# A two-layer decoder trunk on one core: scores of alternating row halves, values as the stationary operand, and gates and branches issued in another order

## The chip, the core and the metric

The kernel runs on one core of a Trainium2 chip. TensorE (PE; PEld is its loading of weights) multiplies, VectorE (DVE) and ScalarE (ACT) do the element-wise work, GpSimd (POOL) a few powers, and SyncE (SP) issues the DMAs. The metric is the device time of one execution in microseconds; lower is better.

## What is computed

Two equal layers over 256 tokens of width 1024, in float32. Cut to what matters here:

```
h    = rms_norm(x);  proj = h @ w_in[l]              # columns of four mixers A, B, C, D, then 4 x 1024 gate columns
yA   = attention over the top 64 keys that an indexer of 8 heads x 32 picks (1 k/v head)
yB   = block attention (one block of 256 keys: plain causal), 4 heads x 64
yC   = g0*compressed + g1*selected blocks + g2*window attention      # 1 k/v head each
yD   = sliding window 128 with a learned sink per head, 2 k/v heads
br_n = y_n @ w_branch[l, n]
x    = x + (sum_n sigmoid(gate_n) * br_n) @ w_out[l]
x    = x + conv_ffn(rms_norm(x))                     # up, causal width-3 convolution, silu * value, down
```

## The kernel before, in words

Every weight matrix comes in chunks of up to 1 MB through three buffers (`raw`); ACT rounds each piece of up to 128x1024 to a short float (`hi`), DVE subtracts it from the original (`lo`), four tiles of each. TensorE then does three fast products per weight tile (`hi` by the high and the low part of the activations, `lo` by the high part), with 128 tokens as the stationary operand and 512 weight columns moving, into PSUM banks `mm0` to `mm3`. The attention itself is in plain float32, which TensorE runs as two records per product.

One layer goes: projections of A, B, D, C; then for each branch n its gate (two halves of 512 columns, 48 fast products each) and its branch product (two halves, 12 each); the output product; up and down of the FFN. While TensorE works on that main stream, the four mixers run beside it: norms, rotations, transposes, and ten calls of `attend` in a layer (A, B and D two each, C four), one for the first 128 queries (t=0, 128 keys) and one for the second (t=1, 256 keys).

`attend` does, for four heads: scores (q as stationary operand, 64 rows of the array per product; heads of even and odd number lie in rows 0 to 63 and 64 to 127) into a bank `sc` for each parity, a maximum on DVE (`attend_max`), exponentials on ACT, transposes of the probabilities through a bank `tr` and copies back (`evac_tr`), and the product with the values. Before, the transposed probabilities are the stationary operand (128x128) and the values (64 columns) move; the result, queries in partitions, is multiplied by 1/denominator on DVE. `y_T` then transposes a mixer's result (four transposes) for the branch product. `indexer` multiplies heads of 32 rows in four row groups, one group after another.

No engine's order is written by hand. Each piece of work is a generator that yields the engine it wants and the values it waits for; `Flow.run` keeps a clock for each engine, prices each instruction with `Eng.cost`, and issues next whatever can start first by these clocks, then by priority. "AV" takes ACT or DVE, whichever is free first. The order is fixed at build time; on the chip each engine works through its own in order. Buffers and banks go round in rings (`mm_r`: 4 banks, `sc_r`: 2, `tr_r`: 2), so an owner must give one back before the next can take it.

Of the kernel before, what the change touches and what calls it, by code (L numbers as in the profile page):

```python
# [9 lines left out]
F32 = mybir.dt.float32  # L10
F32R = mybir.dt.float32r
# [161 lines left out]
class Eng:  # L173
# [6 lines left out]
    def cost(self, m, a, k):  # L180
# [49 lines left out]
def trunk(ctx: ExitStack, tc: tile.TileContext, a, out):  # L230
# [163 lines left out]
    GATES = (0, 1, 2, 3)  # L394
    HID_AT = (0, 1)
    PRIO = (4, 19, 7, 21)
# [6 lines left out]
    for l in range(DEPTH):  # L403
# [7 lines left out]
        for n in GATES:  # L411
            for half in range(2):
# [3 lines left out]
                if (n, half) == HID_AT:  # L416
                    for i in range(2):
                        ap = a["c_cmp_w1"][l, i].rearrange("(c p) h -> p c h", p=128)
                        plan.append(Chunk(ap, (16, 128), []))
                if n == GATES[-1]:  # L420
                    rows_chunk(a["w_branch"][l, n], 0, 2, half * 512, half * 512 + 512)
            if n != GATES[-1]:
# [211 lines left out]
    def attend(t, qT, kblk, kT, vfn, scl, mask, y, needs, sink=None, fin=None, gate=None):  # L634
        nk = 128 * (t + 1)
        Sx = sm = None
        rdf = Fut()
        tx = []
        for par in range(2):
            if par == 0:  # L640
                sxt, sm, sc = yield "PE", needs, [sx_r, sm_r, sc_r]
                Sx = sxt.rearrange("p (h n) -> p h n", h=H)
                mx, nmx, den, es, rd = (sm[k] for k in ("mx", "nmx", "den", "es", "rd"))
            else:
                sc, = yield "PE", [], [sc_r]
            b = 64 * par
            for hh in range(2):
                te = P.matmul(sc[:, hh * nk:hh * nk + nk], qT[b:b + 64, hh, t * 128:t * 128 + 128],
                              kT[b:b + 64, kblk(2 * hh + par), :nk], start=True, stop=True)
            fl.spawn(attend_max(t, sc, te, par, Sx, nk, mask, scl, sink, mx, tx), 8)  # L650
# [14 lines left out]
        fl.spawn(recip(t2, den, rd, gate, rdf), 8)  # L665
        tes = []
        pTt = None
        for g in range(t + 1):
            if g == 0:
                pTt, tb = yield "PE", [te], [pt_r, tr_r]  # L670
                pT = pTt.rearrange("p (h b q) -> p h b q", h=H, b=2)
            else:
                tb, = yield "PE", [], [tr_r]
# [14 lines left out]
        sx_r.give(sxt, tq)  # L688
        ob, = yield "PE", tes, [tr_r]
        op = ob[:, :256].rearrange("p (h d) -> p h d", h=H)  # L690
# [4 lines left out]
        rdb = rd[:, :, None].to_broadcast([128, H, DH])  # L695
        if gate is None:
            yield "DVE", [te, rdf], []
            te = V.tensor_tensor(heads(y)[:, t], op, rdb, op=ALU.mult)
            tr_r.give(ob, te)
        else:  # L700
            otmp, = yield "DVE", [te, rdf], [ot_r]
            te = V.tensor_tensor(otmp, op, rdb, op=ALU.mult)
            tr_r.give(ob, te)
            yield "DVE", [te], []
            te = V.tensor_tensor(heads(y)[:, t], heads(y)[:, t], otmp, op=ALU.add)
            ot_r.give(otmp, te)
        sm_r.give(sm, te)
# [128 lines left out]
    def indexer(t, iqT, ikT, iw, needs, fin, f):  # L836
        nk = 128 * (t + 1)
        mask = tri[:, 256 - nk:]
        ac = acc[t]
        for r4 in range(4):  # L840
            sc, rl = yield "PE", needs, [sc_r, rl_r]
            for g in range(2):
                te = P.matmul(sc[:, g * nk:g * nk + nk], iqT[32 * r4:32 * r4 + 32, g, t * 128:t * 128 + 128],
                              ikT[32 * r4:32 * r4 + 32, 0, :nk], start=True, stop=True)
            yield "ACT", [te], []
            te = A.activation(rl[:, :2 * nk], sc[:, :2 * nk], AF.Relu)
            sc_r.give(sc, te)
            td = te
# [162 lines left out]
    ot_r = Ring([junk[:, :256].rearrange("p (h d) -> p h d", h=H)])  # L1011

# [30 lines left out]
    def nsa_cmp(qT, needs, tvb, cgv, y, y0):  # L1043
# [26 lines left out]
        fl.spawn(cmp_den(tp_, Pv, crd, cgv, crd_f := Fut()), 12)  # L1070
        pTt, tb = yield "PE", [tp_], [pt_r, tr_r]
# [6 lines left out]
        for t in range(NT):  # L1078
            te = P.matmul(tb[:, t * 256:t * 256 + 256], pTt[:, t * 128:t * 128 + 128], vbd.rearrange("p h d -> p (h d)"),
                          start=True, stop=True)  # L1080
        pt_r.give(pTt, te)
        yield "DVE", [te, crd_f], []
        te = V.tensor_tensor(heads(y), tb.rearrange("p (t h d) -> p t h d", t=NT, h=H),
                             crd[:, :, :, None].to_broadcast([128, NT, H, DH]), op=ALU.mult)
# [30 lines left out]
    def merge(mg, ps, rg, te, gate, gf, half, i, old, f):  # L1115
        hs = slice(half * 512, half * 512 + 512)
        for t in range(NT):
            if i == 0:
                yield "DVE", [te, gf], []
# [313 lines left out]
```

## Time and profile before

| | us |
|---|---|
| median of 3 runs | 877.55 (877.33 to 881.88) |
| the profiled execution | 881.64 |
| its span, first to last instruction | 879.8 |
| PE busy | 874.4 (99%) |
| DVE busy | 667.9 (76%) |
| ACT busy | 526.3 (60%) |

The profile is of one execution. "Busy" of PE is modelled from pipelined records: one lasts longer than the time until the next starts, so what a product costs is read from start to start in the timeline.

### The profile page before, as it was taken

How to read it: one execution, taken by the hardware profiler on the slowest of the kernel's cores; microseconds unless marked ns; L12 is line 12 of the kernel's file. 1: busy time of each engine (PE TensorE's matmuls, PEld its weight loads, DVE VectorE, ACT ScalarE, POOL GpSimd, SP SyncE). 2: the span in 40 equal slices, each digit the busy share in tenths (PEclk: the TensorE clock that was granted, in tenths of full speed). 3: DMA queues.
4: the chain of work that ended last, by engine and by line, in shares of the span. 5: the costliest groups of instructions: out<-in, count | busy, mean ns of one | idle time of the engine just before them, and what ended most of it. 6: DMA issues, size and time to landing. Idle time of an engine off the chain costs nothing.

```text
span 879.8 us, 14193 instructions
## 1 busy us (share of the span) xinstructions
PE 874.4 (99%) x5491; PEld 766.2 (87%) x5491; DVE 667.9 (76%) x1301; ACT 526.3 (60%) x895; POOL 34.3 (4%) x31
## 2 busy tenths in 40 slices
PE   9999999999999999999999999999999999999998
PEld 8979887788889999988898888787888999999886
DVE  4779888956768999884457997968476699899642
ACT  5655465555457887764455465646545598888431
POOL 0111002000000000000001111000000000000000
PEclk9999999999999999999999999999999999999999
DMA  7627364235555555555554264542356455565560
GB/s 266 237 87 240 96 239 145 83 127 174 192 176 179 200 191 192 193 168 193 170 172 168 85 205 144 193 144 97 120 184 222 144 192 195 194 201 192 178 215 25
DMA packets 103413, 149.90 MB, mean 170 GB/s; under 512 B 4072, under 2 KB 62258, under 8 KB 103346
## 3 DMA queue, kind: packets, MB, share of 16 engines
q1 hardware_dynamic: 103346, 149.00, 50.6%
q8 instruction: 43, 0.70, 0.3%
q14 instruction: 24, 0.20, 0.1%
HBM read 147.94 MB, written 1.05 MB: 169 GB/s over the span
## 4 chain that ended last, share of the span: by engine, by line
PE 98%; ACT 0%; DMA 0%; SPq 0%; DVE 0%; issue 0%; DVEq 0%
PE mm L212 82%; PE sc L212 8%; PE tr L212 8%; DMA rn<-in_norm_g_dram 0%; ACT f L212 0%; ACT L212 0%; SPq L240 0%; ACT hi L212 0%; DVE x L212 0%; DVEq L1429 0%
## 5 line engine op out<-in xcount | busy, mean ns | idle before, releaser
L212 DVE TENSOR_TENSOR lo<-raw,hi 128x1024 fp32r<-128x1024 f32 (+2 forms) x280 | 328.1, 1177 | 117.2 <-ACT hi L212 113.3
L212 ACT ACTIVATE hi<-raw 128x1024 fp32r<-128x1024 f32 (+2 forms) x280 | 283.3, 1022 | 170.7 <-PE mm L212 143.1
L212 PE MATMUL mm<-hi,ahi 128*128 128x512 f32 (+4 forms) x480 | 178.1, 377 | 0.0
L212 PE MATMUL mm<-hi,alo 128*128 128x512 f32 (+4 forms) x480 | 172.3, 365 | 0.0
L212 PE MATMUL mm<-ahi,hi 128*128 128x256 f32 x640 | 152.3, 279 | 0.0
L212 PE MATMUL mm<-alo,hi 128*128 128x256 f32 x640 | 152.0, 278 | 0.0
L212 PEld LDWEIGHTS mm<-ahi,hi 128*128 128x128 f32 x640 | 120.6, 188 | 0.1
L212 PEld LDWEIGHTS mm<-alo,hi 128*128 128x128 f32 x640 | 120.6, 188 | 0.1
L212 PE MATMUL mm<-lo,ahi 128*128 128x512 f32 (+4 forms) x480 | 118.3, 370 | 0.0
L212 PEld LDWEIGHTS mm<-hi,ahi 128*128 128x128 f32 x480 | 90.7, 189 | 14.9 <-issue 2.7
L212 PEld LDWEIGHTS mm<-hi,alo 128*128 128x128 f32 x480 | 90.8, 189 | 11.2
L212 PEld LDWEIGHTS mm<-lo,ahi 128*128 128x128 f32 x480 | 82.9, 188 | 13.8 <-issue 1.7
L212 PE MATMUL mm<-hi,slotQ 128*128 128x512 f32 x352 | 89.9, 395 | 0.0
L212 PE MATMUL mm<-ahi,lo 128*128 128x256 f32 x640 | 88.1, 278 | 0.0
L212 PEld LDWEIGHTS mm<-ahi,lo 128*128 128x128 f32 x640 | 80.2, 188 | 0.0
L212 PEld LDWEIGHTS mm<-hi,slotQ 128*128 128x128 f32 x352 | 66.1, 188 | 15.3
L212 ACT ACTIVATE f<-f,col 128x256 f32<-128x256 f32 x88 | 48.1, 593 | 14.5 <-DVE f L212 14.0
L212 PE MATMUL mm<-lo,slotQ 128*128 128x512 f32 x176 | 48.7, 395 | 0.0
L212 ACT ACTIVATE f<-f,nmx 128x128 f32<-128x128 f32 (+1 forms) x80 | 35.4, 445 | 9.6 <-DVE nmx L212 9.4
L212 ACT ACTIVATE slotP<-mm,rh 128x512 f32<-128x512 f32 x32 | 20.4, 684 | 33.2 <-PE mm L212 33.0
L212 PE MATMUL sc<-qk 64*128 64x128 f32 (+3 forms) x224 | 39.9, 348 | 0.0
L212 PEld LDWEIGHTS mm<-lo,slotQ 128*128 128x128 f32 x176 | 33.0, 188 | 7.6
(219 smaller groups left out, 1091.7 us busy)
## 6 DMA issues: line engine op xcount, KB each, us to landing
raw<-in_w_up_dram SPq DMA_DIRECT2D x44, 1024.0 KB, 5.0
raw<-in_w_in_dram SPq DMA_DIRECT2D x40, 1024.0 KB, 4.9
raw<-in_w_down_dram SPq DMA_DIRECT2D x20, 1024.0 KB, 4.9
raw<-in_w_out_dram SPq DMA_DIRECT2D x8, 1024.0 KB, 5.2
raw<-in_w_branch_dram SPq DMA_DIRECT2D x6, 1024.0 KB, 5.7
raw<-in_w_in_dram SPq DMA_DIRECT2D x7, 768.0 KB, 6.1
raw<-in_w_in_dram SPq DMA_DIRECT2D x4, 592.0 KB, 4.1
raw<-in_w_in_dram SPq DMA_DIRECT2D x4, 536.0 KB
```

The lines of the kernel that those rows point to most:

```text
L212: fn(*a, **k)
```

## The change

- `attend`: both parities of the scores are issued in one step that takes both `sc` banks, in turn (even, odd, even, odd). The probabilities are divided by the denominator before they are transposed, four instructions on ACT or DVE, which wait for `recip`. The values become the stationary operand (64 columns) and the transposed probabilities move (128 columns); the result has features in partitions, even heads in 0 to 63 and odd heads in 64 to 127, and is copied (or, in C, added) into `y`.
- `y_T` no longer transposes: a copy on ACT and a subtraction on DVE.
- `indexer`: the eight score products in one step, row groups in turn, into four banks (two `sc`, two `tr`).
- `nsa_cmp`: as `attend`, with the same number of products.
- Gates and branches follow a list, `SEQ`: gates 0, 1, 2, then branches 0, 1, 2, then gate and branch 3 by halves. The first gate is written to `mg` itself. Priorities of mixers B, C and D change.
- The planner prices a fast product at 0.446 ns a column, 0.417 before, and divides the price of products in separate strips by their number (`P.side`).

```diff
-                c = 0.417 * n + 2 if a[1].dtype == F32R else 1.67 * max(n, free_size(a[1])) + 2
+                c = 0.446 * n + 2 if a[1].dtype == F32R else 1.67 * max(n, free_size(a[1])) + 2
...
-    GATES = (0, 1, 2, 3)
-    HID_AT = (0, 1)
-    PRIO = (4, 19, 7, 21)
+    SEQ = [("gate", 0, 0), ("gate", 0, 1), ("hidden", 0, 0), ("hidden", 1, 0), ("gate", 1, 0),
+           ("gate", 1, 1), ("gate", 2, 0), ("gate", 2, 1), ("branch", 0, 0), ("branch", 0, 1),
+           ("branch", 1, 0), ("branch", 1, 1), ("branch", 2, 0), ("branch", 2, 1), ("gate", 3, 0),
+           ("branch", 3, 0), ("gate", 3, 1), ("branch", 3, 1)]
+    PRIO = (4, 7, 19, 21)
...
     def y_T(y, yf, yT, f):
-        yT += yield "PE", [yf], [y_r]
-        yield from rows_T(y, [yf], yT[0], 0, f)
+        yT += yield "ACT", [yf], [y_r]
+        te = A.activation(yT[0][0], y, AF.Copy)
+        yield "DVE", [te], []
+        f.t = V.tensor_tensor(yT[0][1], y, yT[0][0].bitcast(F32), op=ALU.subtract)
...
-        for par in range(2):
-            if par == 0:
-                sxt, sm, sc = yield "PE", needs, [sx_r, sm_r, sc_r]
...
-            else:
-                sc, = yield "PE", [], [sc_r]
-            b = 64 * par
-            for hh in range(2):
-                te = P.matmul(sc[:, hh * nk:hh * nk + nk], qT[b:b + 64, hh, t * 128:t * 128 + 128],
+        sxt, sm, *scs = yield "PE", needs, [sx_r, sm_r, sc_r, sc_r]
...
+        for hh in range(2):
+            for par in range(2):
+                b = 64 * par
+                te = P.matmul(scs[par][:, hh * nk:hh * nk + nk], qT[b:b + 64, hh, t * 128:t * 128 + 128],
...
+        for h in range(H):
+            eng, _ = yield "AV", [rdf], []
+            if eng == "ACT":
+                tn.append(A.activation(Sx[:, h, :nk], Sx[:, h, :nk], AF.Copy, scale=rd[:, h:h + 1]))
+            else:
+                tn.append(V.tensor_scalar(Sx[:, h, :nk], Sx[:, h, :nk], rd[:, h:h + 1], None, op0=ALU.mult))
...
-        for h in range(H):
+        for k in range(2):
             for b in range(t + 1):
-                te = P.matmul(op[:, h, :], pT[:, h, b, :], vfn(h, b), start=b == 0, stop=b == t)
+                for par in range(2):
+                    te = P.matmul(op[64 * par:64 * par + 64, k, :], vfn(2 * k + par, b), pT[:, 2 * k + par, b, :],
+                                  start=b == 0, stop=b == t)
...
-            te = V.tensor_tensor(heads(y)[:, t], op, rdb, op=ALU.mult)
+            te = copy_on(eng, yt, op)
...
-            te = V.tensor_tensor(otmp, op, rdb, op=ALU.mult)
...
-            te = V.tensor_tensor(heads(y)[:, t], heads(y)[:, t], otmp, op=ALU.add)
+            te = V.tensor_tensor(yt, yt, op, op=ALU.add)
...
-        for r4 in range(4):
-            sc, rl = yield "PE", needs, [sc_r, rl_r]
-            for g in range(2):
-                te = P.matmul(sc[:, g * nk:g * nk + nk], iqT[32 * r4:32 * r4 + 32, g, t * 128:t * 128 + 128],
+        rgs = [sc_r, sc_r, tr_r, tr_r]
+        bks = yield "PE", needs, rgs
+        P.side = 4
+        for g in range(2):
+            for r4 in range(4):
+                tm = P.matmul(bks[r4][:, g * nk:g * nk + nk], iqT[32 * r4:32 * r4 + 32, g, t * 128:t * 128 + 128],
```

How it moves instructions, at three places of the first layer. The first is TensorE's order at the indexer's scores for t=0 (`qk_88` holds the indexer's q and k, `hi`/`lo` by `ahi`/`alo` are the projection of B beside it); before, and then the piece of the difference:

```order
 L212 MATMUL mm_64<-hi_77,alo 128x512
 L212 MATMUL sc_68<-qk_88 128x128 x2
 L212 MATMUL sc_67<-qk_88 128x256 x2
 L212 MATMUL mm_63<-lo_81,ahi 128x512
 L212 MATMUL mm_64<-lo_81,ahi 128x512
 L212 MATMUL mm_63<-lo_81,ahi 128x512
 L212 MATMUL mm_64<-lo_81,ahi 128x512
 L212 MATMUL sc_68<-qk_88 128x128 x2
```

```order
 L212 MATMUL mm_64<-hi_76,alo 128x512
+L212 MATMUL sc_68<-qk_88 128x128
+L212 MATMUL sc_67<-qk_88 128x128
+L212 MATMUL tr_70<-qk_88 128x128
+L212 MATMUL tr_69<-qk_88 128x128
+L212 MATMUL sc_68<-qk_88 128x128
```

Groups of two products into one bank, spread over the projection, become one run of eight into four banks.

The second is TensorE's order at the last value product of the first layer's attention (`f_2_84` holds transposed probabilities, `slotQ` the projections with the values in them); before, it stands between the halves of gate 2:

```order
 L212 MATMUL mm_63<-lo_79,ahi 128x512
 L212 MATMUL mm_64<-lo_79,ahi 128x512
 L212 MATMUL tr_70<-slotQ,f_2_84 128x64 x8
 L212 MATMUL mm_65<-hi_76,ahi 128x512
 L212 MATMUL mm_65<-hi_76,alo 128x512
```

Of the change, there:

```order
 L212 MATMUL mm_64<-hi_74,yhi_116 128x512
 L212 MATMUL mm_64<-hi_74,ylo_117 128x512
 L212 MATMUL tr_70<-f_2_84,slotQ 64x128 x8
 L212 MATMUL mm_63<-lo_78,yhi_116 128x512
 L212 MATMUL mm_64<-lo_78,yhi_116 128x512
```

It now stands inside branch 1 (`yhi`, `ylo` are a mixer's result), after all of gates 0 to 2 and branch 0; its operands have changed places, and it writes 64 partitions by 128 columns a product.

The third is DVE's order at the merge of branch 1 (`slotP` holds gates, `mg` the sum); before, it is mixed with the maxima of an attention (ISA, and its mx row):

```order
 L212 SCALAR_TENSOR_TENSOR slotP<-slotP,mm_63 128x512
 L212 ISA f_0_82,mx_104<-sc_67,cst,sC 128x128
 L212 ISA mx_104 128x1
 L212 TENSOR_TENSOR mg<-mg,slotP 128x512
 L212 SCALAR_TENSOR_TENSOR slotP<-slotP,mm_64 128x512
```

Of the change:

```order
 L212 SCALAR_TENSOR_TENSOR slotP<-slotP,mm_63 128x512
 L212 TENSOR_TENSOR mg<-mg,slotP 128x512
 L212 SCALAR_TENSOR_TENSOR slotP<-slotP,mm_64 128x512
 L212 TENSOR_TENSOR lo_78<-raw_71,hi_74 128x1024
 L212 TENSOR_TENSOR mg<-mg,slotP 128x512
 L212 TENSOR_TENSOR ylo_117<-slotQ,yhi_116 128x512
 L212 SCALAR_TENSOR_TENSOR slotP<-slotP,mm_65 128x512
```

The merges of branches 1 and 2 now follow each other with only splits of weights between them.

## Rows read from the trace of the kernel before

**Rows 1.** The page, busy time of two engines (us, share of the span).
```profile
PE 874.4 (99%) x5491; PEld 766.2 (87%) x5491; DVE 667.9 (76%) x1301; ACT 526.3 (60%) x895; POOL 34.3 (4%) x31
```
**Rows 2.** The page, the chain that ended last, by engine.
```profile
PE 98%; ACT 0%; DMA 0%; SPq 0%; DVE 0%; issue 0%; DVEq 0%
```
**Rows 3.** Busy us of each engine by stretch, the attention stages and the densest.
```profile
core 0: us, PE busy (x) PEld busy (x) DVE busy (x) ACT busy (x) POOL busy (x), PEclk, DMA share, GB/s
60.00:90.00 30.00, 30.00 (x177) 26.03 (x177) 28.06 (x85) 17.47 (x30) 3.81 (x1) 1.00 0.53 176
30.00:188.00 158.00, 158.00 (x948) 130.04 (x946) 134.14 (x385) 89.21 (x189) 15.63 (x9) 1.00 0.45 152
467.00:621.00 154.00, 153.94 (x927) 126.61 (x926) 129.83 (x377) 85.74 (x184) 13.70 (x8) 1.00 0.45 151
```
**Rows 4.** PE timeline (start, us, count of records): scores and values, t=0.
```profile
154.63 0.71 PE L212 MATMUL sc<-qk 64*128 64x128 f32 x4
155.27 1.10 PE L212 MATMUL tr<-slotQ,f 128*128 128x64 f32 x8
156.21 0.61 PE L212 MATMUL tr<-cst,f 128*128 128x128 f32 x4
156.75 0.71 PE L212 MATMUL sc<-qk 64*128 64x128 f32 x4
...
610.43 1.13 PE L212 MATMUL sc<-qk 64*128 64x256 f32 x4
```
**Rows 5.** PE timeline: two fast products, then scores and values, t=1.
```profile
159.32 0.39 PE L212 MATMUL mm<-hi,yhi 128*128 128x512 f32 x1
159.55 0.39 PE L212 MATMUL mm<-hi,ylo 128*128 128x512 f32 x1
159.87 1.13 PE L212 MATMUL sc<-qk 64*128 64x256 f32 x4
160.93 2.00 PE L212 MATMUL tr<-slotQ,f 128*128 128x64 f32 x16
162.76 0.61 PE L212 MATMUL tr<-cst,f 128*128 128x128 f32 x4
```
**Rows 6.** PE timeline: scores whose two parities follow each other directly.
```profile
82.16 0.72 PE L212 MATMUL sc<-qk 64*128 64x128 f32 x8
82.82 0.96 PE L212 MATMUL mm<-lo,ahi 128*128 128x512 f32 x3
...
88.52 1.14 PE L212 MATMUL sc<-qk 64*128 64x256 f32 x8
89.59 0.66 PE L212 MATMUL tr<-cst,f 128*128 128x128 f32 x4
...
149.21 1.67 PE L212 MATMUL sc<-qk 64*128 64x256 f32 x8
```
**Rows 7.** PE timeline: 16 products in four column strips (the compressor's hidden layer).
```profile
552.91 1.07 PE L212 MATMUL mm<-raw,kr 128*15 128x128 f32 x32
553.90 1.13 PE L212 MATMUL sc<-qk 64*128 64x256 f32 x4
```
**Rows 8.** PE groups by form: indexer scores, and transposes out of the projections' buffer.
```profile
L212 PE MATMUL sc<-qk 32*128 32x256 f32 x32 | 8.8, 394 | 0.0
L212 PE MATMUL sc<-qk 32*128 32x128 f32 x32 | 5.7, 296 | 0.0
L212 PE MATMUL tr<-cst,slotQ 128*128 128x128 f32 x36 | 5.6, 272 | 0.0
```
**Rows 9.** DVE groups by form (busy us, mean ns of one, idle before).
```profile
L212 DVE TENSOR_TENSOR lo<-raw,hi 128x1024 fp32r<-128x1024 f32 x248 | 301.5, 1220 | 110.7 <-ACT hi L212 110.2 <-issue 0.2
L212 DVE TENSOR_TENSOR mg<-mg,slotP 128x512 f32<-128x512 f32 x24 | 16.3, 684 | 0.0
L212 DVE TENSOR_TENSOR junk<-tr,rd 128x256 f32<-128x256 f32 x8 | 3.3, 419 | 2.0 <-PE tr L212 1.3 <-ACT f L212 0.7
L212 DVE TENSOR_SCALAR sel<-acc 128x256 f32<-128x256 f32 x2 | 0.6, 286 | 0.0
```

More of the change, by code (lines that the diff above doesn't have):

```diff
@@ L410, in trunk @@
                 rows_chunk(wi, 4 * kg, 4 * kg + 4, c0, c1)
-        for n in GATES:
-            for half in range(2):
+        for op, n, half in SEQ:
+            if op == "gate":
                 for kg in range(2):
@@ L415, in trunk @@
                     rows_chunk(wi, 4 * kg, 4 * kg + 4, c0, c0 + 512)
[L416 to L422, printed above, removed]
+            elif op == "hidden":
+                ap = a["c_cmp_w1"][l, n].rearrange("(c p) h -> p c h", p=128)
+                plan.append(Chunk(ap, (16, 128), []))
+            elif n == LAST:
+                rows_chunk(a["w_branch"][l, n], 0, 2, half * 512, half * 512 + 512)
+            elif half == 0:
                 ap = a["w_branch"][l, n].rearrange("(k p) n -> p k n", p=128)
@@ L1009, in nsa @@
                                 fin=fin, gate=cgv[:, t, :, 1 + i]), 13 + 2 * i + t)
-    ot_r = Ring([junk[:, :256].rearrange("p (h d) -> p h d", h=H)])
     class Hidden:
@@ L1281, in main, with gate_of, branch_out @@
                         mixer(n, f)
-            gts = None
-            mT = None
+            gts = mT = None
             mf = [Fut() for _ in range(4)]
-            merged = [[Fut(), Fut()] for _ in range(4)]
-            def branch_out(i, half, yT, ytf, pc_, gate, gf):
-                nonlocal mT
+            merged = [[], []]
+            places = [([], o) for o in range(0, 4096, 1024)]
+            gates, yTs, shared = {}, {}, {}
+            def gate_of(n, half):
+                nonlocal gts
+                ps = yield "PE", [], [mm_r] * NT
+                if n == FIRST:
+                    old, dst = [], mg[:, :, half * 512:half * 512 + 512]
+                else:
+                    if gts is None:
+                        gts = one.tile([128, 8 * 512], F32, name="slotP")
+                    old, o = places.pop(0)
+                    dst = gts[:, o:o + 1024].rearrange("p (t n) -> p t n", t=NT)
+                f = Fut()
+                gates[n, half] = dst, f, None if n == FIRST else o
+                for kg in range(2):
+                    ch = next(it)
+                    te = yield from macs(ch, ch.pieces, ps, hget, hfut, 4 * kg, kg == 0, kg == 1)
+                fl.spawn(gate_out(ps, te, rh[l], rhf, old, dst, f), 3)
+            def branch_out(n, half):
+                nonlocal mT
+                yT, ytf = yTs[n]
+                if n == LAST:
+                    pc_ = next(it).pieces[0]
+                else:
+                    if half == 0:
+                        shared[n] = next(it)
+                    pc_ = shared[n].pieces[half]
+                gate, gf, o = gates[n, half]
                 rg = sc_r if half == 0 and all(f.t is not None for f in yf) else mm_r
@@ L1300, in branch_out @@
                         fl.spawn(rows_T(mg[:, :, 128 * k0:128 * k0 + 256], [f], mT, k0, mf[2 * half + j], scale=0.5), 2)
-                return te
-            for i, n in enumerate(GATES):
-                gate, gf = [], []
-                yT, ytf = [], Fut()
-                fl.spawn(y_T(ys[n], yf[n], yT, ytf), 2)
-                for half in range(2):
-                    ps = yield "PE", [], [mm_r] * NT
-                    if gts is None:
-                        gts = one.tile([128, 8 * 512], F32, name="slotP")
-                    o = 1024 * ((2 * i + half) % 4)
-                    gate.append(gts[:, o:o + 1024].rearrange("p (t n) -> p t n", t=NT))
-                    gf.append(Fut())
-                    for kg in range(2):
-                        ch = next(it)
-                        te = yield from macs(ch, ch.pieces, ps, hget, hfut, 4 * kg, kg == 0, kg == 1)
-                    fl.spawn(gate_out(ps, te, rh[l], rhf, [merged[i - 2][half]] if i > 1 else [], gate[half], gf[half]), 3)
-                    if (n, half) == HID_AT:
-                        for j in range(2):
-                            yield from hidden(j, next(it), hid)
-                    if i == 3:
-                        te = yield from branch_out(i, half, yT, ytf, next(it).pieces[0], gate[half], gf[half])
-                if i < 3:
-                    ch = next(it)
-                    for half in range(2):
-                        te = yield from branch_out(i, half, yT, ytf, ch.pieces[half], gate[half], gf[half])
-                y_r.give(yT[0], te)
+            order = [n for op, n, half in SEQ if op == "branch" and half == 0]
+            for i, n in enumerate(order):
+                yTs[n] = [], Fut()
+                fl.spawn(y_T(ys[n], yf[n], *yTs[n]), 2)
+            for op, n, half in SEQ:
+                if op == "gate":
+                    yield from gate_of(n, half)
+                elif op == "hidden":
+                    yield from hidden(n, next(it), hid)
+                else:
+                    yield from branch_out(n, half)
             ps2 = []
```

79 lines of the change are left out of this document (42 added, 37 removed).

## Prediction

> **What bounds the kernel now.** I read the page first. TensorE is busy for 874.4 us of the span, DVE for 667.9 [rows 1], and the chain that ended last is 98% TensorE [rows 2]: no other engine holds it up, so what counts is how much time TensorE's own work takes, and whether it begins to wait. Second, the busy time by stretch, since an average hides the stage that is changed. In the two attention stages (30 to 188 and 467 to 621 us) TensorE is busy all the time, at clock 1.00, while DVE is busy for 134.14 of 158 us (85%) and 129.83 of 154 (84%); in its densest 30 us it reaches 28.06 (94%) [rows 3]. So DVE is the engine that comes next, with some 15% to spare. Third, TensorE's timeline in order of time, where the distance from one start to the next is what a group costs. The longer duration beside it has a tail that overlaps what follows.
>
> **The change part by part.** All of it lies in the attention stages.
>
> *Values.* At t=0 an attend has four products, eight records: 155.27 to 156.21, 0.94 us [rows 4]. At t=1 there are eight, sixteen records: 160.93 to 162.76, 1.83 [rows 5]. There are 20 attends, ten of each: 10 x 2.77 = 27.7 us. Now two products write different halves of the partitions and can run side by side, with 128 columns moving instead of 64. The nearest row is the compressor's hidden layer, which moves 128 columns in strips of the array, four abreast: 32 records in 552.91 to 553.90, 0.99 us, so eight rounds of 0.124 [rows 7]. Two abreast, t=0 takes four rounds (0.50) and t=1 eight (0.99): 10 x 1.49 = 14.9. Entering another shape costs something: a fast product follows the last by 0.23, but scores follow one by 0.32 [rows 5], so 0.09 more, 20 times: 1.8. Gain 27.7 - 14.9 - 1.8 = 11.0. That row has strips of 32 columns; if strips of 64 don't run side by side, a record with 128 columns costs about what one with 64 did (0.117 against 0.124 in these rows), nothing is gained and the 1.8 is lost. I take the 11.0, since the row differs only in width.
>
> *Scores.* They gain only where the parities stand apart now. One group costs 0.64 at t=0 (154.63 to 155.27) and 1.06 at t=1 [rows 4, 5]. But where both follow each other, all eight records take 0.66 (82.16 to 82.82) and 1.07 (88.52 to 89.59) [rows 6]: the two halves of the rows work abreast already, whole. Of the 20 attends, 13 stand together and 7 apart, 14 groups of four records from 154.63 to 610.43 [rows 4]: three at t=0, four at t=1. These save 3 x 0.64 + 4 x 1.06 and seven entries of 0.09: 6.8. A few of the 13 are abreast in part only, as the 1.67 at 149.21 against 1.14 [rows 6]; I put that at 1.2 together. Gain 8.0; the bounds are 0, if taking turns loses what neighbours have, and 8.0.
>
> *Indexer.* Its groups hold TensorE for 8.8 + 5.7 us [rows 8]; less 16 tails of 0.07 (1.13 against 1.06 [rows 5]) that is 13.4, and with 14 entries of 0.09 it is 14.7. Four row groups abreast should cost one group, as two halves did: 0.66 and 1.07 with an entry each, 1.9 a layer, 3.8 in all. Gain 10.9. If only two run abreast, the body is 6.9 and the gain 7.4. I take four, because the column strips of [rows 7] run four abreast.
> The Trainium skill's page "TensorE: Matmul & The Clock Gate" (Part 3, Packing small matmuls) gives 3.07x, not 4x, for four row tiles. By that the indexer would keep 13.4 / 3.07 = 4.4 us and the gain would be about 10; no run here shows four row tiles yet.
>
> *y_T.* 32 of the 36 transposes out of the projections' buffer [rows 8] go, eight groups of four. Such a group takes 0.54 from 156.21 to 156.75 [rows 4], of which 0.09 is the entry of what follows: 8 x 0.45 = 3.6. The copy and the subtraction that stay are as many as before.
>
> *nsa_cmp* has as many products as before: nothing.
>
> Sum: 11.0 + 8.0 + 10.9 + 3.6 = 33.5 us less for TensorE, 16.7 a layer.
>
> *What the others get.* The normalization adds four instructions to each attend: 80, of which the order puts 38 on DVE. The nearest row is a multiplication by a number, 0.286 for 256 columns [rows 9], so at most 10.9. DVE loses 28 multiplications out of PSUM and 8 additions and gets 8 additions back, at 0.42 each [rows 9]: -11.8. A few copies come over from ACT (about ten). For DVE that is nothing to +5 us over two layers, for ACT some 42 instructions more, with 89.21 of 158 us busy in the stage [rows 3]. So the work of DVE stays and the time for it shrinks: by 16.7 a layer, less what the new order gives back. In the first layer the last value product stood before half a gate, branch 2 and gate and branch 3 (48 + 24 + 96 + 24 = 192 fast products), and now stands after half of branch 1's first half (about 160 to come). At 0.23 each that is 7 us more of TensorE's main stream ahead of the end of attention. The stage is then 158 - 16.7 + 7 = 148 us, and DVE's 134 are 91% of it, below the 94% that it reaches now. It fits, but not everywhere.
>
> *Waits that I expect.* First, the transposes wait for the reciprocal and for the first two normalizations (some 0.3 us each), where they waited for the exponentials alone; fast products stand in front of them, but TensorE takes its list in order, so each late one stops it. Second, the branches in a row: for half a branch, TensorE needs 12 x 0.23 = 2.8 us and DVE four merges of 0.68 and a split of 1.22 [rows 9], 3.9. Over the four halves of branches 1 and 2 DVE falls back by about 4.5; four `lo` tiles ahead and six banks cover most of it. From the two I take 3.5 us a layer, 7 in all, between 0 and 15 (below).
>
> So the profiled execution's 881.64 would be 881.6 - 33.5 + 7 = 855. The median of the runs, 877.55, is 4.1 below the profiled one, and I forecast for it: **851 us**.
>
> **The rivals.**
> *DVE becomes the bound.* The Trainium skill's page "TensorEngine Tiling (Array Packing)" (Performance Considerations, PSUM Bottleneck) warns of this: packing speeds up TensorE and not the emptying of PSUM. As a mechanism here: if DVE can't be filled beyond 90% over a whole stage, with its short dependent steps, then 134 us take 149, and without the 7 us moved ahead the stage gains 9 instead of 16.7. Two layers: 18 less, 859; if it can't pass 85%, nothing is gained. For it speaks that DVE's share is 94% only where the indexer's selection fills it; against it that the wait is then on a fixed order which was laid out with DVE's costs in it. 859 to 869.
> *The values don't run side by side* (the bound above): 33.5 - 12.8 - 7 = 14, so 864.
> *No new waits at all:* 33.5, so 844.
> *No change:* the gains are eaten by waits of about the same size, 873 to 882. It needs DVE stuck at today's 85%.
> *Slower:* an attend has three to five steps on TensorE, some 80 over the kernel. The new price of a product lets the plan put such a step where its input is just ready, where before the plan ran ahead of TensorE and inputs lay waiting. If each is late by 0.42 us, the 33.5 are gone; at 0.6 it is 48, 892. That [rows 2] shows no share for any other engine says how much slack these steps have today; against it stands that entries of 0.09 and the tails aren't in the plan, so TensorE comes later than planned.
>
> **How the numbers follow.** The forecast as worked out, with waits of 3 to 11 us (847 to 856): 0.50. No waits (842 to 847): 0.15. DVE as the bound: 0.15. Values not abreast: 0.06. No change: 0.08. Slower: 0.06. The range 842 to 867 leaves out the last two and the edges of the others. A measurement of this kernel tells about 0.5% (4.4 us) from no change. Faster by more: 0.50 + 0.15 + 0.15 + 0.06 = 0.86; within: 0.08; slower: 0.06.
>
> **What would show it.** In the profile after: value groups of 0.5 and 1.0 us from start to start, scores of eight records always at 0.66 and 1.07, the indexer's sixteen records in the same times; no transposes out of the projections' buffer but four. DVE's share in the attention stages near 90%, and the end of attention at about 178 us. The chain should stay TensorE, with a per cent or two for DVE or ACT. The prediction is wrong if DVE shows a large share of the chain inside these stages, or if the groups keep their old length.

## The result, and the profile after

| | before | after |
|---|---|---|
| median | 877.91 us (877.33 to 881.88, 4 runs) | 854.75 us (851.93 to 856.96, 4 runs) |
| the profiled execution | 881.64 | 856.96 |
| its span | 879.8 | 855.1 |
| TensorE busy / span less busy | 874.4 / 5.4 | 844.3 / 10.8 |

The ratio is 0.972, with a 95% interval of 0.969 to 0.975; it is taken over all runs, and so differs a little from that of the two medians. The forecast was 851, between 842 and 867.

The last line of the table splits the result into the two halves of the forecast's sum: TensorE has 30.1 us less work, and it waits for 5.4 us more; 24.7 us remain, which is the difference of the two spans. First the page of the kernel after: the busy times, and the chain of waits by engine.

```profile
PE 844.3 (99%) x5459; PEld 735.7 (86%) x5459; DVE 674.2 (79%) x1327; ACT 542.1 (63%) x943; POOL 32.2 (4%) x31
...
PE 92%; DMA 3%; DVE 2%; ACT 2%; issue 1%; SPq 0%; DVEq 0%; ACTq 0%
```

TensorE is still the bound, but its share of the chain fell from the 98% of [rows 2] to 92%. That is not 6% of waiting. In front of a single wait of 1.2 us at 45.21 the chain leaves TensorE and follows DVE, ACT and the loads of the weights through most of the first 45 us (from there come DMA's 3%), while TensorE is idle for 10.8 us in the whole span. Next its timeline in the first layer: start and duration in us, then what it does, and in brackets the idle time and who ended it.

```profile
46.51 0.38 PE L212 MATMUL sc<-qk 32*128 32x128 f32 x2
...
46.96 0.28 PE L212 MATMUL tr<-qk 32*128 32x128 f32 x2
47.17 1.20 PE L212 MATMUL mm<-lo,ahi 128*128 128x512 f32 x4
...
53.79 0.48 PE L212 MATMUL sc<-qk 32*128 32x256 f32 x2
...
54.87 0.50 PE L212 MATMUL mm<-hi,ahi 128*128 128x512 f32 x1
...
95.89 0.72 PE L212 MATMUL sc<-qk 64*128 64x128 f32 x8
96.54 0.50 PE L212 MATMUL mm<-hi,ahi 128*128 128x512 f32 x1
...
97.66 0.66 PE L212 MATMUL tr<-f,kvA 128*64 128x128 f32 x8
98.24 0.51 PE L212 MATMUL mm<-hi,ahi 128*128 128x512 f32 x1
...
99.29 1.08 PE L212 MATMUL mm<-lo,ahi 128*128 128x512 f32 x4
101.89 0.66 PE L212 MATMUL tr<-cst,f 128*128 128x128 f32 x4 [1.52 <-ACT f L212]
102.48 1.06 PE L212 MATMUL mm<-raw,kr 128*15 128x128 f32 x32
103.47 0.66 PE L212 MATMUL tr<-cst,f 128*128 128x128 f32 x4
104.06 1.07 PE L212 MATMUL mm<-raw,kr 128*15 128x128 f32 x32
105.14 0.36 PE L212 MATMUL tr<-cst,hsum 128*128 128x15 f32 x2
105.44 1.09 PE L212 MATMUL tr<-f,kvA 128*64 128x128 f32 x16
106.46 1.13 PE L212 MATMUL sc<-qk 64*128 64x256 f32 x8
107.53 0.40 PE L212 MATMUL tr<-cst,hsum 128*128 128x15 f32 x2
107.77 0.48 PE L212 MATMUL mm<-hi,ahi 128*128 128x512 f32 x1
```

Read from start to start. The indexer's sixteen records, four row groups in turn, take 0.66 us (46.51 to 47.17) and 1.08 (53.79 to 54.87). Scores of eight records take 0.65 (95.89 to 96.54) and 1.07 (106.46 to 107.53). Values take 0.58 (97.66 to 98.24) and 1.02 (105.44 to 106.46), where [rows 4] and [rows 5] have 0.94 and 1.83. The last ten rows show something else: from 99.29 to 107.77 the list holds four fast products at the start and none after them. All that is between are steps of the mixers and the compressor's hidden layer (`mm<-raw,kr`), and in front of the first of them TensorE waits. I call such a piece a *stretch without fast products* (from the start of the last fast product to the start of the next); this one is 7.8 us long. The longest of what TensorE waited for in the kernel after, by releaser (us in total, times, longest; three more are of 0.4 to 0.7 us each):

```profile
PE tr L212 <- ACT f L212: 1.9, 2, 1.5
PE mm L212 <- DVE kr L212: 1.2, 1, 1.2
PE tr L212 <- DVE kr L212: 1.2, 1, 1.2
PE sc L212 <- DVE f L212: 1.0, 1, 1.0
```

The same view of the kernel before has two waits, 1.0 for DVE's `f` and 0.4 for a DMA. New are those of the transposes for ACT's `f` (the divided probabilities) and for `kr`: once in front of the indexer's transposes (`tr<-cst,kr`), once in front of the hidden layer (`mm<-raw,kr`), whose input mixer C makes in that buffer. Last, the busy time of the engines in the first layer's attention stage (PE, PEld, DVE, ACT, POOL; then the clock):

```profile
30.00:178.00 148.00, 144.84 (x929) 117.51 (x929) 132.12 (x388) 98.76 (x215) 13.83 (x9) 1.00 0.49 164
```

DVE is busy for 132.12 of 148 us, 89%.

The longest new wait, 1.52 us at 101.89, has two parts. ACT's timeline in front of it (`mg<-mm,rh` is the first gate on its way out of its bank, `f<-f,rd` the divisions):

```profile
100.17 1.27 ACT L212 ACTIVATE mg<-mm,rh 128x512 f32<-128x512 f32 x2 [1.44 <-PE mm L212]
101.33 1.30 ACT L212 ACTIVATE f<-f,rd 128x256 f32<-128x256 f32 x3
```

DVE had the reciprocal ready at 100.10. But ACT had first waited for TensorE's gate and then copied it, 1.2 us, before it came to its three divisions.

### The profile page after: what moved, and what is told of

Its sections match the earlier page's. It is cut to its first block, busy times and chain, and to the rows that moved or that the text cites. A ratio compares the mean times of both kernels' runs of the same rounds, so it can differ in the third digit from the quotient of the medians.

```text
span 855.1 us, 14191 instructions
## 1 busy us (share of the span) xinstructions
PE 844.3 (99%) x5459; PEld 735.7 (86%) x5459; DVE 674.2 (79%) x1327; ACT 542.1 (63%) x943; POOL 32.2 (4%) x31
## 4 chain that ended last, share of the span: by engine, by line
PE 92%; DMA 3%; DVE 2%; ACT 2%; issue 1%; SPq 0%; DVEq 0%; ACTq 0%
PE mm L212 79%; PE sc L212 7%; PE tr L212 6%; DMA raw<-in_w_in_dram 2%; DVE lo L212 1%; DMA f<-in_a_qk_g_dram 1%; ACT hi L212 1%; DMA rn<-in_norm_g_dram 0%; ACT f L212 0%; SPq L240 0%; ACT mg L212 0%; DVE f L212 0%; DVE kr L212 0%; DVE kn L212 0%; ACT L212 0%
## 5 line engine op out<-in xcount | busy, mean ns | idle before, releaser
L212 ACT ACTIVATE qk<-f,col 128x256 f32<-128x256 f32 x88 | 39.2, 495 | 0.0
L212 DVE SCALAR_TENSOR_TENSOR f<-f,col,f 128x254 f32<-128x254 f32 x88 | 38.4, 477 | 0.0
```

Of the source, the lines that this page charges most:

```text
L212: fn(*a, **k)
```

## The experiments

All are compared with the kernel before on the same chip. The first eight ask which part brings the gain. The last four ask why the parts don't add up. In the `diff` fences of this section the lines are shortened to what changes.

| kernel | median (lowest to highest), us | ratio to before, 95% | span, profiled | TensorE busy | span less busy | longest stretch without fast products, layer 0 / 1 |
|---|---|---|---|---|---|---|
| before | 877.91 (877.33 to 881.88) | | 879.8 | 874.4 | 5.4 | 6.1 / 4.8 |
| after | 854.75 (851.93 to 856.96) | 0.972 [0.969, 0.975] | 855.1 | 844.3 | 10.8 | 7.8 / 4.8 |
| scores_alone | 872.68 (868.76 to 873.06) | 0.989 [0.987, 0.991] | 871.2 | 864.3 | 6.9 | 3.6 / 5.6 |
| indexer_alone | 872.30 (867.92 to 872.76) | 0.988 [0.986, 0.991] | 866.2 | 857.3 | 8.9 | 8.9 / 6.1 |
| values_alone | 884.98 (878.20 to 885.99) | 1.004 [1.002, 1.006] | 882.7 | 868.0 | 14.7 | 25.7 / 11.2 |
| order_alone | 891.46 (884.11 to 894.26) | 1.010 [1.005, 1.016] | 886.9 | 877.1 | 9.8 | 8.1 / 4.8 |
| old_seq | 861.65 (858.96 to 865.32) | 0.979 [0.975, 0.984] | 857.2 | 846.5 | 10.7 | under 2.6 / 14.3 |
| old_pace | 874.55 (870.73 to 878.08) | 0.993 [0.991, 0.996] | 868.9 | 846.3 | 22.6 | 11.2 / 30.6 |
| no_division | 856.13 (853.67 to 858.26) | 0.972 [0.968, 0.976] | 856.3 | 848.9 | 7.4 | 3.4 / 3.3 |
| switch_priced | 866.79 (861.61 to 867.49) | 0.983 [0.979, 0.988] | 865.2 | 848.6 | 16.6 | 18.6 / 7.3 |
| values_paced | 876.27 (875.05 to 882.53) | 0.997 [0.995, 0.999] | 876.2 | 864.2 | 12.0 | 3.5 / 3.5 |
| pace_alone | 884.19 (883.44 to 888.24) | 1.008 [1.005, 1.010] | 886.2 | 877.3 | 8.9 | 4.8 / 4.8 |
| branch0_first | 863.37 (859.69 to 870.24) | 0.983 [0.979, 0.986] | 858.4 | 843.6 | 14.8 | 9.5 / 3.0 |
| pace_452 | 871.73 (866.69 to 872.16) | 0.991 [0.988, 0.994] | 870.4 | 852.9 | 17.5 | 18.4 / 10.2 |

The ratios are again taken over all runs. The stretches are those in the attention stages, read from TensorE's timeline as above. Before was timed beside each group of runs: 881.67 and 881.72 beside the first eight, 880.67 beside the last four. Some 4 us of such differences, and of the busy times, are not the kernels' (see the last section).

**Each packed part alone.** Theory A: the gain is TensorE's shorter groups. Theory B: it is the order of gates and branches and the new price. The first kernel is the one before with the scores in turn (the lines of `attend` that take both banks), the second has only the new `indexer`, the third the new values, the division and the `y_T` without transposes, with the old scores.

```diff
# scores_alone, in attend
-        for par in range(2): ...; sc, = yield "PE", [], [sc_r]
+        sxt, sm, *scs = yield "PE", needs, [sx_r, sm_r, sc_r, sc_r]
# indexer_alone, in indexer
-        for r4 in range(4): sc, rl = yield "PE", needs, [sc_r, rl_r]
+        bks = yield "PE", needs, [sc_r, sc_r, tr_r, tr_r]
# values_alone, in attend, y_T, nsa_cmp
-                te = P.matmul(op[:, h, :], pT[:, h, b, :], vfn(h, b), ...)
+                te = P.matmul(op[64 * par:64 * par + 64, k, :], vfn(2 * k + par, b), pT[:, 2 * k + par, b, :], ...)
```

> The kernel before with the scores of both parities in one step, in turn, and nothing else. If the gain is TensorE's shorter groups (theory A), the profile after has its score groups at 17.1 us from start to start against 24.5 before, so 7 us less: about 871 (0.992). If the gain comes from the order of gates and the new price (theory B), this gives no change, 876 to 879. All four products now wait for both banks at once; if that wait costs more than it saves, slower than 879.

> The kernel before with the indexer's eight products in one step in four banks, and nothing else. Theory A: its groups go from 12.5 to 3.4 us and fourteen entries of 0.09 to four: 9 to 10 less, about 868 (0.989). Theory B: no change, 876 to 879. The two transposing banks are held by it for that long, so other mixers could come later and eat some of it.

> The kernel before with the values as stationary operand, the probabilities normalized before the transposes, no transposes in y_T, and nothing else (scores, indexer, order of gates and price as before). Theory A: value groups from 26.3 to 16.1 us and transposes of 3 us gone, 1.8 of entries added: 11 less, less 2 for waits on the normalization: about 868 (0.990). Theory B: no change or slower, since the transposes wait longer: 876 to 882.

Scores and indexer brought 9 us each (881.67 to 872.68 and 872.30). The values, on which the largest term of the forecast rested, brought nothing: 884.98. Yet 18 of their 20 groups were as short there as in the kernel after (0.59 and 1.02 us); the other two, of 1.12 and 1.91, fell into the lower clock shown below. TensorE's timeline shows where the time went:

```profile
105.25 1.08 PE L212 MATMUL mm<-lo,ahi 128*128 128x512 f32 x4
107.26 1.67 PE L212 MATMUL sc<-qk 64*128 64x256 f32 x8 [0.93 <-DVE mx L212]
111.32 1.14 PE L212 MATMUL tr<-cst,f 128*128 128x128 f32 x4 [2.39 <-ACT f L212]
...
116.59 1.97 PE L212 MATMUL tr<-cst,f 128*128 128x128 f32 x8 [1.83 <-ACT f L212]
...
125.47 1.70 PE L212 MATMUL mm<-raw,kr 128*15 128x128 f32 x32 [0.89 <-DVE kr L212]
```

From 105.93 (the last of the four in the first line) to 131.60 no fast product starts. Each step of one attend waits for DVE and ACT to finish the last. And the clock falls, as the windows of the same stretch show (the third number from the end is the granted clock):

```profile
108.00:112.00 4.00, 1.61 (x9) 0.85 (x7) 3.57 (x16) 3.26 (x14) 2.18 (x1) 1.00 0.76 262
112.00:116.00 4.00, 2.62 (x14) 1.54 (x14) 3.43 (x9) 3.46 (x9) 0.00 (x0) 0.51 0.00 0
116.00:120.00 4.00, 3.36 (x16) 2.42 (x18) 3.56 (x12) 3.19 (x8) 0.00 (x0) 0.50 0.23 57
...
128.00:132.00 4.00, 4.00 (x39) 2.57 (x38) 2.18 (x10) 0.00 (x0) 1.05 (x1) 0.50 0.79 263
```

Before the fall, from 108 to 112 us, TensorE was busy for 1.61 of 4 us; then it was granted the lower of its two levels (0.50, 1.2 GHz), for most of 20 us. So this kernel paid 9.3 us of additional idle time and about 7 us of work at half the clock (the busy time of each window from 112 to 136 us, times what its clock lacks of 1). Adding the 7 back, its TensorE work is some 13.5 us less than before; the forecast's terms for values and `y_T` are 14.6, and the same groups of the kernel after are 13.4 us shorter than before (see the account of the prediction).

**The order alone.** The kernel after, with `attend`, `indexer`, `y_T` and `nsa_cmp` of before: only `SEQ`, the priorities, the first gate's place and the price are new.

> The kernel after with attend, indexer, y_T and nsa_cmp as before: only the list of gates and branches, the priorities, the first gate in the sum's place and the new price are left. Theory A: TensorE has the same work, 876 to 881. Theory B: most of the gain, 855 to 865.

891.46, 1.0% slower than before, outside both expectations. Theory B falls: without the shorter groups the new order costs time. Of the 7.1 us between the profiled executions 4.4 are idle time. Its longest wait is in front of the hidden layer, 2.42 us for `kr` at 123.13 us.

**The old order, and the old price, in the changed kernel.**

```diff
# old_seq
+    SEQ = gates 0, hidden, branch 0, gate 1, branch 1, gate 2, branch 2, gate and branch 3 by halves; PRIO = (4, 19, 7, 21)
# old_pace
-                c = 0.446 * n + 2 if a[1].dtype == F32R else ...
+                c = 0.417 * n + 2 if a[1].dtype == F32R else ...
```

> The kernel after with gates and branches in turn as before (gate 0, hidden, branch 0, gate 1, branch 1, ...) and the old priorities of the mixers; packing and price as after. If the three gates ahead serve the gain (theory B), it loses 5 to 15 us, 860 to 870, as TensorE comes to a branch before its mixer is done. Theory A: within 3 of the kernel after, 852 to 858.

> The kernel after with the old price of 0.417 a column. If the true price makes the plan tight and is what lets TensorE wait (1.7 us at 100, 1.3 at 522 of the trace after), the old one gives 2 to 4 back: 851 to 853. If the true price serves the gain (theory B): slower than after by 3 or more, 858 and up. Theory A: within 2.

By the ratios, the old order costs 0.7% of the 2.8% gained (0.979 for 0.972), the old price 2.1% (0.993). The first is at the edge of what can be told: the two intervals meet at 0.975, and the profiled executions differ by 2.1 us. The second is clear, and it went the way of theory B, against the expected gain of 2 to 4. Theory A in its simple form, in which terms add up, falls too: the parts alone sum to 9 + 9 - 3 - 10, and together they make 23. In the second layer of old_pace, TensorE's timeline has the longest stretch of all, 30.6 us:

```profile
520.72 0.71 PE L212 MATMUL sc<-qk 64*128 64x128 f32 x8
524.84 1.12 PE L212 MATMUL tr<-f,kvA 128*64 128x128 f32 x8 [3.41 <-ACT f L212]
...
536.05 0.70 PE L212 MATMUL tr<-cst,kr 128*128 128x128 f32 x4 [1.49 <-DVE kr L212]
...
547.31 3.11 PE L212 MATMUL mm<-raw,kr 128*15 128x128 f32 x64 [3.96 <-DVE kr L212]
550.35 0.80 PE L212 MATMUL mm<-hi,ahi 128*128 128x512 f32 x1
```

It ends as the one of values_alone did: with the hidden layer, behind which the fast products stand. And as there, the lower clock comes with it (the number after POOL's count):

```profile
520.00:524.00 4.00, 1.43 (x13) 0.87 (x11) 3.16 (x6) 4.00 (x10) 0.00 (x0) 1.00 0.02 4
524.00:528.00 4.00, 2.90 (x16) 1.97 (x16) 2.94 (x15) 3.28 (x10) 0.00 (x0) 0.50 0.55 183
```

**The division left out.** The kernel after without the four divisions by the denominator; its output lacks the normalization. The buffer of the small sums is given back at the end of `attend`.

```diff
-            if eng == "ACT":
-                tn.append(A.activation(Sx[:, h, :nk], Sx[:, h, :nk], AF.Copy, scale=rd[:, h:h + 1]))
-            else: ...
+        tn = [te] * H
```

> The kernel after without the division of the probabilities by the denominator in attend (the output lacks it); the transposes wait for the exponentials, as before. If the waits of TensorE after the change come from this longer chain, 4 to 6 us less, 849 to 851. If they come from ACT's order (an ACT instruction that waits for TensorE stands ahead of the division), the same, as the place in the line stays taken: 853 to 855, or a little less from 42 instructions fewer on ACT.

856.13, the same ratio as the kernel after (0.972). In the profiles the idle time is 3.4 us less (7.4 for 10.8) and the busy time 4.6 more. About 4 of these 4.6 are the FFN stage, which ran at its longer pace in both layers here and in one there. So the division chain may cost some 3 us, or its absence gave the planner a luckier order; this run doesn't tell the two apart.

**A price for changing the shape.** The planner adds 150 ns when a product's strips differ from those of the one before, which is meant to bring its clock nearer to TensorE's.

```diff
-            return c / self.side * (1 if ...)
+            self.was, new = self.side, 150 * (self.side != self.was)
+            return new + c / self.side * (1 if ...)
```

> The kernel after whose planner adds 150 ns for each change between whole and split array. In the profile after, packed groups take 0.2 us longer than the plan has them, so TensorE comes later than planned, and ACT instructions that wait for it block what stands behind them (the wait at 100 us). If that is the cause, the plan becomes truer and 2 to 5 us come back: 850 to 853. If not, within 2 of the kernel after.

866.79, or 1.7% faster than before where the kernel after is 2.8% faster, with a stretch of 18.6 us at the hidden layer. Both expectations missed: to price one more cost gave a worse order.

**Is it the stretch at the hidden layer?** From these eight runs I formed theory C: the work that the packing saves is always saved, and what differs is whether TensorE's list has a long stretch at the hidden layer. The hidden layer stands in the main stream after gate 0 and needs mixer C's `kr`; where C is late, the planner fills TensorE with steps of the mixers, and these are a dependent chain.

```diff
# values_paced: values_alone with
-                c = 0.417 * n + 2 ...
+                c = 0.470 * n + 2 ...
# pace_alone: before with 0.446; pace_452: after with 0.452
# branch0_first: after with
-("hidden", 0, 0), ("hidden", 1, 0), ("gate", 1, 0), ... ("branch", 0, 0), ("branch", 0, 1),
+("branch", 0, 0), ("branch", 0, 1), ("hidden", 0, 0), ("hidden", 1, 0), ("gate", 1, 0), ...
```

> The kernel before with the values as stationary operand, as in the run with this part alone (884.98 us), and one number more: the planner prices a fast product at 0.470 ns a column instead of 0.417. What TensorE computes is the same, only the order differs. Theory C (the hole): that run lost because TensorE's list has a stretch without any fast product, 25.7 us long in layer 0 and 11.2 in layer 1, both ending at the 64 records of the compressor's hidden layer, which stands in the main stream and waits for mixer C; each step of the mixers in it waits for the one before. In the order planned here no such stretch is left, so the gain of the values and of the missing transposes (26.3 to 16 and 3 us) appears: 862 to 868. Rival D (the values themselves cost it: division and copies on engines that are late): the waits come back elsewhere and the time stays at 880 to 886.

> The kernel before with the price 0.446 instead of 0.417 ns a column and nothing else. Theory C: before has one stretch of 4.7 us without fast products at the hidden layer, of which 3.9 us or so is work; the price removes it, worth 0 to 2 us: 875.5 to 878.5. Rival E (a true price is worth something by itself, as the 18 to 20 us between the changed kernel with either price suggest): 858 to 868.

> The changed kernel with branch 0 issued right after gate 0 and before the hidden layer (gates 1 and 2 then follow, then branches 1 and 2). Theory C: the 24 products of branch 0 cover the wait for mixer C; no stretch without fast products is left in the planned order (the changed kernel has one of 7.8 us in layer 0 and 4.8 in layer 1), so the 4 to 5 us of new waits mostly go: 849 to 853. Rival D: the waits come from the division chain and stay, 854 to 857. Rival F: three gates ahead of the first branch matter for themselves, and this gives part of them up: 858 to 862.

> The changed kernel with the price 0.452 instead of 0.446 ns a column, 1.3% more. Theory C: the order planned with it has a stretch without fast products at the hidden layer in both layers, of 76 and 64 products where the changed kernel has 54 and none as long; by the runs so far such stretches (81 and 65 products in the values alone, 108 and 56 with the price 0.417) cost 12 to 22 us: 864 to 874. Rival E (the closer the price is to the truth the better, smoothly): a product takes 0.23 us for 512 columns, 0.449 ns a column, and 0.452 is as near to it as 0.446, so 853 to 857.

pace_452 is as theory C has it: 1.3% more on one price, the stretches come (18.4 and 10.2 us), and of the 2.8% gained 0.9% is left. Theory E, that a truer price helps smoothly, falls with it; it falls with pace_alone as well, which is not faster but 0.8% slower (6.4 us between the two profiled executions, of which 4.8 are the pace of the FFN). Theory C's 875.5 to 878.5 for pace_alone is missed as well: its idle time is 3.5 us more than before.

values_paced is half a success. The stretches went, as planned, and the ratio fell from 1.004 to 0.997; but 876.27 us is well above the 862 to 868 expected. Its work is 10.2 us less than before, its idle time 6.6 more. The largest wait is another one now:

```profile
PE tr L212 <- DVE qr L212: 3.4, 4, 1.9
```

That is the pattern of the forecast's rival *slower*: transposes issued where, in the plan, their input is just ready. A price of 0.470 is above the pace of the trace (0.23 us for 512 columns, 0.45 ns each), so TensorE is there early. That the price is what makes it early is argued; the waits are shown. So theory C explains where the time of the worst orders goes, and not that an order without such stretches is free of waits.

branch0_first missed, and its expectation had the order wrong: the trace has stretches in layer 0, of 8.0 us in front of branch 0 and of 9.5 in front of the hidden layer.

```profile
PE mm L212 <- DVE kr L212: 3.6, 1, 3.6
PE mm L212 <- ACT yhi L212: 1.5, 1, 1.5
```

Branch 0 stands there before mixer A's result (`yhi`) is ready, and the hidden layer still waits for `kr`. Its idle time is 14.8 instead of 10.8. Its busy time, 843.6, looks like that of the kernel after, but two differences cancel in it: the FFN ran at the shorter pace in both layers, and part of the attention at the lower clock. It doesn't decide between the theories, but it suggests the use of three gates ahead of the branches: what stands in front of a branch is time for its mixer. No kernel run here beats the one after.

What separates these kernels from the kernel after can be read from the profiled executions, in us. "Lower clock" is half of TensorE's busy time in the stretches in which it was granted 0.50 (17.1 us long together in old_pace, 10.2 in pace_452 and in switch_priced, 6.8 in branch0_first; in the other two and in the kernel after there is none before the last 3 us). "FFN" is the time of all its products of 256 columns from start to start, 244.8 us in the kernel after.

| kernel | span | idle time | lower clock | FFN |
|---|---|---|---|---|
| old_pace | +13.8 | +11.8 | +7.9 | -4.8 |
| pace_452 | +15.3 | +6.7 | +4.5 | +4.0 |
| switch_priced | +10.1 | +5.8 | +4.6 | -0.5 |
| branch0_first | +3.3 | +4.0 | +3.4 | -4.5 |
| old_seq | +2.1 | -0.1 | 0 | -0.4 |
| no_division | +1.2 | -3.4 | 0 | +4.0 |

In the first four, the waits, the lower clock that comes with them and the FFN's pace are the whole difference, to 1.1 us. The FFN's pace is probably not the order's doing: the executions of one kernel lie about as far apart (last section). Of TensorE's waits, 15.0 of 18.7 us lie in the two long stretches of old_pace, 9.0 of 10.8 in those of values_alone, but only 7.8 of 13.5 in pace_452 and 7.5 of 12.7 in switch_priced: the stretches are the largest part of the loss, not all of it.

## Why the prediction was right, step by step

- *Values*, 11.0 us: the mechanism is right, the gain is 10.2. The forecast had groups of 0.50 and 0.99 with an entry of 0.09; they take 0.58 and 1.02, 16.1 us for all twenty. Strips of 64 columns run abreast as those of 32 do in [rows 7]. What is too large is the count of before. The rows 0.94 and 1.83 of [rows 4, 5] were taken for all groups, but both stand right behind scores. Six of ten at t=0 take 0.81 to 0.83, and six of ten at t=1 take 1.70 to 1.73, as these do in the kernel before; all twenty take 26.3 us, not 27.7.

```profile
164.85 1.00 PE L212 MATMUL tr<-slotQ,f 128*128 128x64 f32 x8
165.66 0.70 PE L212 MATMUL mm<-lo,yhi 128*128 128x512 f32 x2
...
120.10 1.89 PE L212 MATMUL tr<-slotQ,f 128*128 128x64 f32 x16
121.80 0.48 PE L212 MATMUL mm<-hi,ahi 128*128 128x512 f32 x1
```

- *Scores*, 8.0: right. Always 0.65 and 1.07, as 0.66 and 1.07 were read from [rows 6]: 17.1 us instead of 24.5, and some entries besides. scores_alone gained 9.0.
- *Indexer*, 10.9: the groups are right, 0.66 and 1.08, or 3.5 us for the four, where 3.8 were counted with entries. Before, they took 12.5 us from start to start and not the 13.4 that the busy time less its tails gave (three pairs of groups stood together already), so the groups save 9.1. indexer_alone gained 9.4, with 3.5 us more idle time than before.
  The Trainium skill's page "TensorE: Matmul & The Clock Gate" (Part 3, Packing small matmuls) gives 3.07x for four row tiles, at 512 columns; the sum by it, an estimate, was 4.4 us for the indexer. The trace doesn't agree: 12.5 us became 3.5, which is 3.6x, and at the 128 and 256 columns of this kernel four row groups take what two halves take (0.66 and 1.08 for 0.65 and 1.07).
- *y_T*, 3.6: the transposes out of the projections' buffer are gone but for the four expected, which were 36 in [rows 8]. The eight groups had taken 3.2 us: most took 0.35, not the 0.45 counted.
- *The sum*, 33.5: 30.1 by the two pages. The four kinds of groups, from start to start in the two traces, give 10.2 + 7.4 + 9.1 + 3.2 = 29.9, so what is missing lies in these terms. The groups after have the sizes forecast; those of before were counted 2.7 us too long, and some 1.5 us of entries were to go with the scores and the indexer that hardly show: the fast products that carry the entries, those of the FFN's first half left out, take 516.9 us before and 516.2 after.
- *What the others get*, nothing to 5 us for DVE: 6.3 (667.9 to 674.2), and 15.8 for ACT. The forecast took 28 multiplications out of PSUM from DVE, at 0.42; there were 20 of that size, and two of 512 columns. It did no harm, since TensorE stayed the bound.
- *Waits*, 7 between 0 and 15: 5.4. The size was right; the place was not. The step named two causes. Of the division chain two waits are seen, 1.9 us together, of which the longer one, at 101.89, is in part ACT's copy of a gate; leaving the divisions out made the idle time 3.4 us less, but in an order of its own. The branches in a row cost nothing that shows in the list of TensorE's waits. Instead there are two waits of 1.2 us for `kr`, in front of the indexer's transposes and of the hidden layer, which the forecast did not name. That the sum of the waits came so near is in part luck: with a price of 0.417 or 0.452 the same products are idle for 22.6 or 17.5 us instead of 10.8, and nothing in the forecast could tell these orders apart.
- *Profile against median*: the forecast took 4.1 us off, because before was profiled 4.1 above its median. After was profiled 2.2 above its own. Profile against profile, 855 was forecast and 856.96 measured; the rest of the 3.75 us between 851 and 854.75 is this step. The near hit of 855 has two errors that partly cancel, 3.4 us too much gain and 1.6 too much waiting.
- *DVE near 90%* in the stage: 89%, against the 85% of [rows 3]. The rival in which DVE becomes the bound did not come as an average. It came in places: where fast products run out, the chain through DVE and ACT sets the time.
- *End of attention at about 178 us*: the last values of the first layer run from 181.77 to 182.79, so 4 to 5 us later.
- *The rival "slower"* had 0.06. The runs make it larger than that: in values_alone and values_paced new idle time of 9.3 and 6.6 us ate most of the gain, and an order drawn with 0.417 or 0.452 keeps 0.7 or 0.9% of the 2.8%. It came otherwise than the rival had it, not as 80 steps each late by 0.4 us, but as few and longer waits, in values_alone most of them inside two stretches. The forecast read the change's order only at three places and did not look for runs of TensorE's list without fast products, which its order shows before any run. That was the view to take.

## What to carry to other kernels

In this kernel, products that use half or a quarter of the array's rows, or half of its columns, cost together little more than one of them alone, when they are issued in turn into separate banks or separate halves of the partitions. What they save can be read beforehand from neighbours in the trace; count every group of before, since the same group takes longer behind one neighbour than behind another. Whether the time follows depends on the order: look through the bottleneck engine's list for long runs without independent work, since there every short wait of the other engines counts in full and the clock may fall on top. Where a planner draws the order, a price changed by 1.3% moved the time by more than 1% (11 of the 15.3 us of pace_452, the rest being the FFN's pace), so a part tried alone is measured together with the order that it happened to get.

## Unexpected in the hardware

**The same products at two paces, at a granted clock of 1.00.** In the FFN's first half TensorE does nothing but products of 256 columns, the same ones in both layers and in all kernels. Windows of 40 us of before (first two lines), after, indexer_alone and no_division, layer 0 and layer 1 of each:

```profile
300.00:340.00 40.00, 40.00 (x342) 40.00 (x342) 36.06 (x53) 32.55 (x53) 0.00 (x0) 1.00 0.55 182
720.00:760.00 40.00, 40.00 (x356) 40.00 (x355) 37.42 (x53) 33.56 (x53) 0.00 (x0) 1.00 0.63 207
```

```profile
300.00:340.00 40.00, 40.00 (x355) 40.00 (x355) 38.35 (x56) 33.62 (x54) 0.00 (x0) 1.00 0.62 205
720.00:760.00 40.00, 40.00 (x342) 40.00 (x341) 35.78 (x50) 31.43 (x49) 0.00 (x0) 1.00 0.58 187
```

```profile
300.00:340.00 40.00, 40.00 (x355) 40.00 (x355) 38.69 (x57) 33.92 (x55) 0.00 (x0) 1.00 0.63 208
720.00:760.00 40.00, 40.00 (x355) 40.00 (x355) 37.34 (x54) 32.97 (x54) 0.00 (x0) 1.00 0.60 197
```

```profile
300.00:340.00 40.00, 40.00 (x342) 40.00 (x341) 36.51 (x53) 32.48 (x51) 0.00 (x0) 1.00 0.58 189
720.00:760.00 40.00, 40.00 (x342) 40.00 (x341) 35.87 (x52) 31.87 (x51) 0.00 (x0) 1.00 0.57 185
```

It is 355 products or 342, a difference of 4%, or about 4 us over a stage of some 120; the stage keeps nearly the same pace throughout. One layer, both or neither can have the longer one: from start to start, the products of 256 columns of both layers take 240.0 to 240.3 us in three of the fourteen profiled executions, 244.0 to 244.8 in eight and 248.8 to 248.9 in three. Times of a kernel fall into groups about 4 us apart (before 877.33, 877.55 and 881.88; after 851.93, 852.81 and 856.69, 856.96), as if the pace were drawn for each execution; with one profile for each kernel that is likely and not shown, and the cause stays open. Before and after were both profiled with one long stage, so their 24.7 us are free of it; the 4 us do stand in some medians of the table.
